# The mixers of a two-block transformer kernel: the written order of TensorE starts at the value projections, second-half gate values between the u blocks, spatial products last

## The chip, the cores and the metric

One core of a Trainium2 chip runs the whole kernel. The metric is the device time of one execution in microseconds (us), as the median of several runs. TensorE (PE) multiplies matrices into accumulator banks, VectorE (DVE) and ScalarE (ACT) read the banks and compute elementwise, GpSimd (POOL) computes elementwise on the main on-chip memory alone, SyncE (SP) issues the loads. Each engine works through its own queue in order and waits on semaphores for the others.

## The reference, cut to what matters

The kernel computes two stacked models in single precision for 512 tokens of width 1024. The change lies in the two layers of the second one, in the first part of each layer (here called the mixer):

```
a = rms_norm(h, pre_mix_g)
zq, zkc, zvc, zks, zvs, zkw, zvw, zg, zu, zv = split(a @ w_in)
q = rope(zq);  k_sel = rope(zks);  k_win = rope(zkw)
kc, vc = compress(zkc), compress(zvc)        # blocks of 32 tokens -> gelu(. @ w1 + b1) @ w2 + b2
kc = rope(kc)
attn = g0 * softmax(q kc) vc + g1 * softmax(q k_sel) v_sel + g2 * softmax(q k_win) v_win
u = gelu(zu);  v = layer_norm(gelu(zv))      # v: tokens x 512
mlp = u * (tril(w_s) @ v + b_s)              # per group of 64 columns, in chunks of 128 tokens
mix = concat(rms_norm(attn), rms_norm(mlp)) @ w_o
h = h + rms_norm(mix)
```

## The kernel before

Activations lie with features on partitions: a tile `[128, 8, 512]` holds 8 blocks of 128 features of 512 tokens. Each weight block (128 x 1024, 512 KB) is loaded, and split into a high part (`whi`, ScalarE, L246) and a rest (`wlo`, VectorE, L249). A product is three matmuls per pair of blocks (high x high, high x low, low x high): a block product is 8 steps of three matmuls, 24 in all.

`mixer_in` makes everything that the attention needs: first two token tiles of the gate values `v` (with GELU and layer norm in `gln_evac`), the keys, the compressed hidden layer `ph`, the queries, then the two value projections (`proj(12 + b)`) with their transposes (vtr), the hidden layer's GELU (`hb`) and transposes (htr), the compressed keys (pkc, then a chain of small operations to `kcst`) and compressed values (pvc to `vcz`), and the transposed attention gates (gtr to `gt`). Up to there a scheduler that works on a timeline of its own chooses the order of TensorE.

From there on TensorE's order is written out by hand: inside `manual_schedule` its instructions go out in the order in which the code issues them. What was issued before it can still be placed between them, and all other engines keep the scheduler's order. `nsa` goes through 16 attention units `(n, rp, b)`: query block `n` of 128 tokens (0 to 3), two head pairs `rp`, two branches `b`; here they are counted 0 to 15. Each unit issues scores of a first and a second group (L1558, L1560; VectorE takes the row maxima `nm`, ScalarE the exponentials, VectorE scales `p`), and transposes (pt, L571) and weighs (o, L580) the unit before. `nsa_compressed` (tile `pc`) comes once per query block.

Between these pieces `slot(ns)` issues *fill*: so many nominal nanoseconds of dense matmuls from the generator `fill`, with what was overdrawn carried on as a debt. A generator that yields `None` has nothing to give. The fill runs through `rest` (four u blocks with GELU; the remaining token tiles 2 and 3 of the gate values; first-half spatial products `spatial(i, 0)`), `rest2` (`spatial(i, 1)`), and the output projection's first half `out["half"]`. A step of three 512-column matmuls counts 681 ns, one of 256 columns 360 ns, a spatial product 1200 ns. `slot.side(...)` runs small steps, one for each slot: `mix_norm` squares and adds, lets some slots pass, and then issues the column sums (rsc, L312), a power on GpSimd (`rcol`, L316), transposes (rsb, L320) and the scaling. Matmul banks: two "mm", three "s", two "pt", one "o".

```
        def rest(wq, slot):                       # L1400
            for j in range(4):
                p = self.bk("mm", [128, S])
                yield from self.mm3_steps(p, next(wq), ax)
                self.gelu2(u[:, j, :], p, gp.tile([128, S], F32, name="gmt", tag="gmt", bufs=2))
                if j % 2:
                    yield spatial(j // 2, 0)
```

Of the kernel before, what the change touches and what calls it, by code (L numbers as in the profile page):

```python
# [10 lines left out]
F32 = mybir.dt.float32  # L11
# [3 lines left out]
AF = mybir.ActivationFunctionType  # L15
# [191 lines left out]
class _K:  # L207
# [927 lines left out]
    def mixer(self, l, at):  # L1135
# [11 lines left out]
        nc.gpsimd.memset(vcz, 0.0)  # L1147
        order = [d[f"w_in{l}"][2 + j] for j in range(4)] + [d[f"w_zv{l}"][0, k] for k in range(4)]
        order += [d[f"wo{l}"][m] for m in range(8)] * 2
        with ExitStack() as sl_, ExitStack() as sg:  # L1150
            gp = self.pool(sg, "mixg", side="right")
            with ExitStack() as s2:
                rest, rest2 = self.mixer_in(l, self.pool(s2, "mixe"), gp, u, qst, kst, kcst, vv, vcz, gt)
            lp = self.pool(sl_, "mixl")
            out = {}

            def fill(wq):
                yield from rest(wq, slot)
                while slot.sides or "ao" not in out:
                    yield None  # L1160
                yield from rest2(slot)
                sg.close()
                out["half"], out["after"] = self.mixer_out(l, self.pool(sl_, "mixf", side="right"))
                yield from out["half"](wq, HALVES[0])
                while "last" not in out:
                    yield None
                yield from out["half"](wq, HALVES[1])

            wq = self.wqueue(order)
            slot = _Slots(fill(wq))  # L1170
            with self.tc.manual_schedule(engines={mybir.EngineType.PE}):
                for hf in self.nsa(lp, qst, kst, kcst, vv, vcz, gt, cmask, slot):
                    slot.side(self.mix_norm(l, "attn_g", self.ao, 0, hf, True))
                    out["ao"] = True
# [19 lines left out]
                self.up = self.group([wu[i] for i in range(self.GROUP)], ("mm", "mm", "s", "s", "s", "pt", "pt"), slot=slot)  # L1194
                assert not slot.sides
        self.tap(f"hm{l}", self.h)

    GROUP = 7

    def mix_norm(self, l, gain, src, k0, hf, quick=False):  # L1200

# [23 lines left out]
    def mixer_in(self, l, at, gp, u, qst, kst, kcst, vv, vcz, gt):  # L1225
# [114 lines left out]
        for r in range(4):  # L1340
            q_ = roped(proj(8 + r) if r else gr[8], 0.125)
            compress(r)
            for g in range(2):
                x, y = (slice(0, 64), slice(64, 128)) if g == 0 else (slice(64, 128), slice(0, 64))
                nc.scalar.copy(qst[x, 2 * r + g, :], q_[x, :])
                nc.vector.tensor_sub(qst[y, 2 * r + g, :], q_[x, :], qst[x, 2 * r + g, :])
        for b in range(2):
            v_ = ev("v_")
            nc.scalar.copy(v_, proj(12 + b))
            p = ptt("vtr", [128, 4, 128])  # L1350
            for t in range(4):
                nc.tensor.transpose(p[:, t, :], v_[:, 128 * t:128 * t + 128], self.ident)
            nc.vector.tensor_copy(vv[b], p)
# [30 lines left out]

        def spatial(i, hf):

            p = self.bk("mm", [128, 2, 2, 128])
            for j in range(2):
                for c in range(2):
                    for e in range(2):  # L1390
                        g = 4 * i + 2 * j + e
                        nc.tensor.matmul(p[64 * e:64 * e + 64, j, c, :], v[:, 2 * hf + c, 64 * g:64 * g + 64], ws[:, g, :],
                                         start=True, stop=True)
            t = gp.tile([128, 2, 2, 128], F32, name="gmt", tag="gmt", bufs=2)
            nc.vector.tensor_tensor(t, p, bs[:, 2 * i:2 * i + 2, None, :].to_broadcast([128, 2, 2, 128]), op=ALU.add)
            x = u[:, 2 * i:2 * i + 2, HALVES[hf]].rearrange("p j (c t) -> p j c t", c=2)
            nc.gpsimd.tensor_mul(x, x, t)
            return 1200

        def rest(wq, slot):  # L1400
            for j in range(4):
                p = self.bk("mm", [128, S])
                yield from self.mm3_steps(p, next(wq), ax)
                self.gelu2(u[:, j, :], p, gp.tile([128, S], F32, name="gmt", tag="gmt", bufs=2))
                if j % 2:
                    yield spatial(j // 2, 0)
            slot.side(self.mix_norm(l, "mlp_g", u[:, :, HALVES[0]], 4, 0))
            pss = [self.bk("mm", [128, S]) for _ in range(2)]
            for kq in range(4):
                w = next(wq)  # L1410
                for t, p in zip((2, 3), pss):
                    for k2 in range(2):
                        k = 2 * kq + k2
                        for i, (a, b) in enumerate(((0, 0), (0, 1), (1, 0))):
                            nc.tensor.matmul(p, self.a[a][:, k, 128 * t:128 * t + 128], w[b][:, 512 * k2:512 * k2 + 512],
                                             start=k == 0 and i == 0, stop=k == 7 and i == 2)
                        yield 681
            for t, p in zip((2, 3), pss):
                gln_evac(t, 0, p)

        def rest2(slot):
            for i in range(2):
                yield spatial(i, 1)
            slot.side(self.mix_norm(l, "mlp_g", u[:, :, HALVES[1]], 4, 1))

        return rest, rest2

# [29 lines left out]
    def nsa(self, at, qst, kst, kcst, vv, vcz, gt, cmask, slot):  # L1457
# [5 lines left out]
        for unit in units + [None]:  # L1463
# [41 lines left out]

    FILL = (2700, 2700, 3400, 3000)

# [214 lines left out]
```

## Time and profile before

| | us |
|---|---|
| median of 3 runs | 2364.74 (2364.59 to 2366.53) |
| the profiled execution's own time | 2362.37 |
| its span | 2360.5 |
| TensorE busy in the span | 2237.1 |
| VectorE / ScalarE / GpSimd busy | 1701.1 / 1140.2 / 519.6 |

Times of rows are counted from the start of the span. PE is the matmuls, PEld the weight loads of TensorE, which run beside them. "idle before" is the time an engine stood still ahead of an instruction, with what ended it. The granted clock is 1.00 at 2.4 GHz and 0.50 at 1.2 GHz.

### The profile page before, as it was taken

Reading aid. Unit: us, or ns where it says so; the run is one execution under the profiler, and the core shown is the slowest. Engines: PE = TensorE matmul, PEld = TensorE weight load, DVE = VectorE, ACT = ScalarE, POOL = GpSimd, SP = SyncE. Lnnn points to the kernel's source line nnn. Section 1 sums busy time; section 2 is a strip of 40 time slices with the busy share of each in tenths; the row PEclk is TensorE's granted clock in tenths of the full one; section 3 lists DMA queues with packets and bytes.
Section 4 is the critical chain, followed back from the end, with each engine's and each line's share of the span. In section 5 each row is a group of like instructions: output and inputs, shape, how many; then the busy total and the mean of one; then the engine's idle time right before and its main releaser. Section 6 shows DMA issues by size and latency. Waiting matters only on the chain.

```text
span 2360.5 us, 37236 instructions
## 1 busy us (share of the span) xinstructions
PE 2237.1 (95%) x14372; PEld 1941.6 (82%) x14372; DVE 1701.1 (72%) x2922; ACT 1140.2 (48%) x2105; POOL 519.6 (22%) x556
## 2 busy tenths in 40 slices
PE   7999999999999989897999999999987999999998
PEld 5877788888888888665898889998865798888998
DVE  5898656846888878776787665668957688666558
ACT  3534444643443434455664444555445665444454
POOL 0110010312444344113121110133203131111004
PEclk9999999999999999998999999999988999999999
DMA  7443134432212344311253235655411143333664
GB/s 286 134 151 99 37 104 132 141 124 82 62 63 63 113 152 130 132 37 46 81 170 105 92 95 157 181 185 163 176 53 45 43 157 126 96 98 112 176 195 134
DMA packets 83746, 279.03 MB, mean 118 GB/s; under 512 B 9584, under 2 KB 14704, under 8 KB 83568
## 3 DMA queue, kind: packets, MB, share of 16 engines
q1 hardware_dynamic: 83568, 276.64, 36.7%
q8 instruction: 113, 1.85, 0.3%
q14 instruction: 65, 0.53, 0.1%
HBM read 274.51 MB, written 2.10 MB: 117 GB/s over the span
## 4 chain that ended last, share of the span: by engine, by line
PE 75%; DVE 13%; ACT 4%; issue 3%; POOL 3%; DMA 2%; SPq 0%; DVEq 0%; ACTq 0%; POOLq 0%
PE mm L279 28%; PE bg L279 23%; PE s L279 3%; DVE wlo L249 2%; PE o L580 2%; PE s L924 2%; PE pt L571 2%; PE bg L845 2%; PE pt L279 1%; PE s L1558 1%; DMA w<-in_w_ada 1%; ACT whi L246 1%; PE s L845 1%; PE bg L1659 1%; DVE ada_p L403 1%
## 5 line engine op out<-in xcount | busy, mean ns | idle before, releaser
L246 ACT CAST whi<-w 128x1024 fp32r<-128x1024 f32 (+1 forms) x436 | 449.1, 1033 | 555.5 <-PE mm L279 249.0
L249 DVE TENSOR_TENSOR wlo<-w,whi 128x1024 fp32r<-128x1024 f32 (+1 forms) x420 | 522.7, 1246 | 223.6 <-ACT whi L246 221.7
L279 PE MATMUL bg<-a,whi 128*128 128x512 f32 x1344 | 415.9, 391 | 0.2 <-ACT whi L246 0.2
L279 PEld LDWEIGHTS bg<-a,whi 128*128 128x128 f32 x1344 | 252.3, 188 | 54.6 <-ACT whi L246 1.0
L279 PE MATMUL mm<-hx,whi 128*128 128x512 f32 x864 | 275.6, 399 | 3.4 <-DVE sga L682 3.0
L279 PE MATMUL bg<-a,wlo 128*128 128x512 f32 x672 | 262.2, 391 | 2.0 <-DVE wlo L249 2.0
L279 PE MATMUL mm<-fh,whi 128*128 128x256 f32 x1408 | 252.7, 282 | 0.0
L279 PEld LDWEIGHTS mm<-fh,whi 128*128 128x128 f32 x1408 | 217.2, 189 | 0.2
L279 PE MATMUL mm<-fh,wlo 128*128 128x256 f32 x704 | 198.9, 284 | 0.6 <-DVE wlo L249 0.6
L279 PEld LDWEIGHTS mm<-hx,whi 128*128 128x128 f32 x864 | 157.9, 190 | 33.1 <-DVE sga L682 3.2
L279 PE MATMUL mm<-a,whi 128*128 128x256 f32 (+1 forms) x768 | 169.8, 317 | 0.0
L279 PE MATMUL mm<-hx,wlo 128*128 128x512 f32 x432 | 169.7, 393 | 0.0
L279 PEld LDWEIGHTS bg<-a,wlo 128*128 128x128 f32 x672 | 126.6, 188 | 29.8 <-DVE wlo L249 3.1
L1611 POOL TENSOR_TENSOR cv<-cv 128x512 f32<-128x512 f32 x44 | 61.5, 1398 | 386.2 <-DVE cv L1598 386.2
L1598 DVE SCALAR_TENSOR_TENSOR cv<-q,cols,cv 128x511 f32<-128x511 f32 (+1 forms) x176 | 134.5, 767 | 2.5
L279 PEld LDWEIGHTS mm<-fh,wlo 128*128 128x128 f32 x704 | 132.6, 189 | 1.0 <-DVE wlo L249 1.0
L279 PEld LDWEIGHTS mm<-a,whi 128*128 128x128 f32 x768 | 124.0, 196 | 7.1 <-issue 4.2
L1605 DVE TENSOR_TENSOR q<-bg,rr 128x512 f32<-128x512 f32 x74 | 51.1, 691 | 107.6 <-PE bg L279 107.6
L279 PE MATMUL mm<-a,wlo 128*128 128x256 f32 (+1 forms) x384 | 117.8, 307 | 0.6 <-DVE wlo L249 0.6
L279 PE MATMUL mm<-hc,whi 128*128 128x256 f32 x576 | 108.6, 287 | 2.3 <-ACT k L813 2.2
L316 POOL TENSOR_TENSOR rcol<-rcol,mhalf 128x2 f32<-128x2 f32 x33 | 24.3, 736 | 348.4 <-DVE rcol L315 348.4
L571 PE MATMUL pt<-ident,p 128*128 128x128 f32 x496 | 72.8, 285 | 29.4 <-DVE p L1577 20.8
(465 smaller groups left out, 4999.8 us busy)
## 6 DMA issues: line engine op xcount, KB each, us to landing
w<-in_wup SPq DMA_DIRECT2D x102, 512.0 KB, 3.5
w<-in_wdn SPq DMA_DIRECT2D x64, 448.0 KB, 3.5
w<-in_w_ada SPq DMA_DIRECT2D x48, 512.0 KB, 3.7
w<-in_w_c SPq DMA_DIRECT2D x48, 512.0 KB, 3.5
w<-in_w_in SPq DMA_DIRECT2D x38, 512.0 KB, 4.7
w<-in_wo SPq DMA_DIRECT2D x32, 512.0 KB, 3.5
w<-in_wdn SPq DMA_DIRECT2D x32, 512.0 KB, 3.6
w<-in_wpg SPq DMA_DIRECT2D x32, 512.0 KB, 3.8
```

Of the source, the lines that this page charges most:

```text
L246: self.nc.scalar.copy(hi[:, :c], w)
L249: eng.tensor_sub(lo[:, :c], w, hi[:, :c])
L279: self.nc.tensor.matmul(ps, w[a][:, (k - k0) * c:(k - k0 + 1) * c], x[b](k), start=first and n == 0, stop=last and n == 3 * len(ks) - 1)
L316: nc.gpsimd.tensor_tensor(col, col, self.mhalf[:, :nt], op=ALU.pow)
L403: nc.vector.scalar_tensor_tensor(t, w, 1.0, self.srow[i], op0=ALU.mult, op1=ALU.mult, accum_out=sums[:, j, i:i + 1])
L571: nc.tensor.transpose(pt[:, c:c + 128], P[g][:, i, kb * 128:(kb + 1) * 128], self.ident)
L580: self.nc.tensor.matmul(o[64 * g:64 * g + 64, 2 * rp:2 * rp + 2, :].rearrange("p a b -> p (a b)"), vt[:, keys[kb], 64 * g:64 * g + 64], pb ...
L845: nc.tensor.matmul(p, xf(k, a, t), w[b][:, 512 * k2:512 * k2 + 512], start=k == 0 and i == 0, stop=k == 7 and i == 2)
L924: nc.tensor.matmul(s_[:, c, :], lhs(c), rhs(c), start=True, stop=True)
L1598: nc.vector.scalar_tensor_tensor(t[:, s:], p[:, :S - s], cw(i), t[:, s:], op0=ALU.mult, op1=ALU.add)
L1605: nc.vector.tensor_mul(q, p, self.rr)
L1611: nc.gpsimd.tensor_mul(a, a, b)
```

## The change

The written order now begins before the value projections, and their two banks are taken from "s"; htr, vtr, pkc, pvc and gtr follow in a fixed order, with two slots of 1300 ns of fill behind the value transposes. The fill goes u0, u1, gate values of tiles 2 and 3, u2, u3, then all four spatial products; `rest2` is gone, and the output projection starts once the side steps of both mlp halves are over. Unit 0's second slot is 4500 instead of 3500, the third entry of `FILL` 4000 instead of 3400. `mix_norm` waits two slots instead of three for the mlp halves and the first attention half, four for the second. Four multiplications by 0.5 on GpSimd (`w2k`, `w2v`, `tri`, `bs`) go; `ht` is copied with a scale of 0.5, and the mlp half, now twice as large, is normalised with four times the epsilon.

```diff
-        order = [d[f"w_in{l}"][2 + j] for j in range(4)] + [d[f"w_zv{l}"][0, k] for k in range(4)]
+        order = [d[f"w_in{l}"][2 + j] for j in (0, 1)] + [d[f"w_zv{l}"][0, k] for k in range(4)]
+        order += [d[f"w_in{l}"][2 + j] for j in (2, 3)]
         order += [d[f"wo{l}"][m] for m in range(8)] * 2
...
-            def fill(wq):
+            def fill(rest):
+                wq = self.wqueue(order)
                 yield from rest(wq, slot)
                 while slot.sides or "ao" not in out:
                     yield None
-                yield from rest2(slot)
                 sg.close()
...
+            with ExitStack() as s2:
+                steps = self.mixer_in(l, self.pool(s2, "mixe"), gp, u, qst, kst, kcst, vv, vcz, gt)
+                slot = self.slot = _Slots(fill(next(steps)))
+                region = self.tc.manual_schedule(engines={mybir.EngineType.PE})
+                region.__enter__()
+                now(steps)
...
-                    slot.side(self.mix_norm(l, "attn_g", self.ao, 0, hf, True))
+                    slot.side(self.mix_norm(l, "attn_g", self.ao, 0, hf, True, 4 if hf else 2))
...
-    def mix_norm(self, l, gain, src, k0, hf, quick=False):
+    def mix_norm(self, l, gain, src, k0, hf, quick=False, wait=2):
-        for _ in range(3):
+        for _ in range(wait):
             yield
-        pr = yield from self.rstd_steps([sq[0][:, 0, :]], 256, self.mean512, NORM_EPS, tmp, "pt")
+        pr = yield from self.rstd_steps([sq[0][:, 0, :]], 256, self.mean512, NORM_EPS * (1 if quick else 4), tmp, "pt")
...
-        for w2 in (w2k, w2v):
-            nc.gpsimd.tensor_scalar(w2, w2, 0.5, None, op0=ALU.mult)
-        nc.gpsimd.tensor_scalar(tri, tri, 0.5, None, op0=ALU.mult)
         nc.gpsimd.tensor_mul(ws, ws, tri[:, None, :].to_broadcast([128, 8, 128]))
-        nc.gpsimd.tensor_scalar(bs, bs, 0.5, None, op0=ALU.mult)
...
+        def rest(wq, slot):
+            def ublock(j):
+                p = self.bk("mm", [128, S])
+                yield from self.mm3_steps(p, next(wq), ax)
+                self.gelu2(u[:, j, :], p, gp.tile([128, S], F32, name="gmt", tag="gmt", bufs=2))
+            for j in range(2):
+                yield from ublock(j)
+            pss = [self.bk("mm", [128, S]) for _ in range(2)]
...
+            for t, p in zip((2, 3), pss):
+                gln_evac(t, 0, p)
+            for j in range(2, 4):
+                yield from ublock(j)
+            for hf in range(2):
+                for i in range(2):
+                    yield spatial(i, hf)
+                slot.side(self.mix_norm(l, "mlp_g", u[:, :, HALVES[hf]], 4, hf))
+        yield rest
+        pv = []
         for b in range(2):
-            v_ = ev("v_")
-            nc.scalar.copy(v_, proj(12 + b))
-            p = ptt("vtr", [128, 4, 128])
...
+            pv.append(proj(12 + b, lambda: self.bk("s", [128, S])))
         hb = at.tile([128, 256], F32, name="hb")
...
+        vs = [ev("v_") for _ in range(2)]
+        nc.scalar.copy(vs[0], pv[0])
         p = ptt("htr", [128, 2, 128])
...
-        nc.scalar.copy(ht, p)
+        nc.scalar.activation(ht, p, AF.Copy, scale=0.5)
+        nc.scalar.copy(vs[1], pv[1])
+        for b in range(2):
+            p = ptt("vtr", [128, 4, 128])
+            for t in range(4):
+                nc.tensor.transpose(p[:, t, :], vs[b][:, 128 * t:128 * t + 128], self.ident)
+            nc.vector.tensor_copy(vv[b], p)
+            self.slot(1300)
         p = ptt("pkc", [128, 64])
...
-                slot(fill if last else 3500)
+                slot(fill if last else 4500)
...
-    FILL = (2700, 2700, 3400, 3000)
+    FILL = (2700, 2700, 4000, 3000)
```

## Rows read from the trace of the kernel before

**Rows 1.** The page: span, and busy time of each engine.

```profile
span 2360.5 us, 37236 instructions
...
PE 2237.1 (95%) x14372; PEld 1941.6 (82%) x14372; DVE 1701.1 (72%) x2922; ACT 1140.2 (48%) x2105; POOL 519.6 (22%) x556
```

**Rows 2.** Stretches of both mixers: length, busy us (instructions), clock, DMA share, GB/s.

```profile
968.75:1155.10 186.35, 158.37 (x1055) 119.30 (x1056) 123.82 (x285) 102.02 (x248) 35.36 (x39) 0.93 0.18 57
1703.54:1889.90 186.36, 157.84 (x1058) 119.21 (x1058) 123.04 (x284) 102.28 (x249) 35.12 (x39) 0.93 0.17 57
```

**Rows 3.** Waits of TensorE in the first mixer: total us, times, longest.

```profile
PE mm L1392 <- POOL v L1296: 11.1, 2, 7.2
PE pt L571 <- DVE p L1577: 10.1, 4, 6.5
...
PE mm L1415 <- DVE gmt L1395: 0.8, 1, 0.8
```

**Rows 4.** Stretches of the first mixer: three holes, each followed by low clock.

```profile
990.90:997.85 6.95, 0.43 (x6) 0.35 (x5) 4.25 (x18) 3.73 (x14) 0.00 (x0) 0.80 0.17 64
997.85:1002.00 4.15, 4.15 (x15) 3.49 (x15) 1.50 (x8) 1.39 (x5) 0.00 (x0) 0.52 0.00 0
...
1010.40:1013.31 2.91, 0.00 (x1) 0.01 (x1) 2.91 (x8) 1.22 (x6) 1.26 (x1) 0.79 0.39 139
1013.31:1018.90 5.59, 5.59 (x19) 3.80 (x19) 3.65 (x16) 2.22 (x7) 1.34 (x2) 0.50 0.00 0
...
1077.70:1089.50 11.80, 0.69 (x4) 0.29 (x4) 7.15 (x18) 3.09 (x5) 9.18 (x10) 0.61 0.14 44
1089.50:1093.80 4.30, 4.30 (x24) 2.81 (x24) 1.25 (x2) 0.64 (x2) 1.27 (x1) 0.50 0.00 0
```

**Rows 5.** The same stretches of the second mixer.

```profile
1726.46:1733.55 7.09, 0.01 (x2) 0.03 (x1) 4.34 (x20) 3.73 (x14) 0.00 (x0) 0.67 0.13 51
1733.55:1738.60 5.05, 5.05 (x19) 3.79 (x19) 2.25 (x11) 1.39 (x5) 0.00 (x0) 0.50 0.00 0
...
1746.78:1749.70 2.92, 0.00 (x0) 0.00 (x1) 2.92 (x8) 1.23 (x6) 1.26 (x1) 0.95 0.37 149
1749.70:1752.50 2.80, 2.80 (x12) 2.57 (x13) 1.29 (x5) 1.63 (x4) 0.67 (x1) 0.50 0.00 0
...
1812.90:1824.66 11.76, 0.69 (x5) 0.30 (x5) 7.11 (x18) 3.08 (x5) 9.14 (x10) 0.56 0.16 45
1824.66:1829.00 4.34, 4.34 (x32) 3.06 (x34) 1.57 (x3) 0.67 (x2) 1.28 (x1) 0.63 0.00 0
```

**Rows 6.** Timeline of TensorE, first mixer: start, busy us, operation, idle before.

```profile
883.05 0.69 PE L320 MATMUL rsb<-ident,rcol 128*128 128x128 f32 x2 [2.72 <-POOL rcol L316]
...
979.36 0.56 PE L1558 MATMUL s<-kst,qst 128*128 128x128 f32 x4
...
989.42 0.55 PE L1364 MATMUL pkc<-ht,w2k 128*128 128x64 f32 x4
...
1061.65 0.59 PE L1558 MATMUL s<-kst,qst 128*128 128x384 f32 x2
...
1070.30 0.60 PE L571 MATMUL pt<-ident,p 128*128 128x128 f32 x4
...
1152.81 0.58 PE L312 MATMUL rsc<-mean,msq 128*128 128x1 f32 x4 [1.49 <-DVE msq L1207]
```

**Rows 7.** Timeline of VectorE, first mixer.

```profile
993.33 0.22 DVE L254 TENSOR_TENSOR kcst<-kc,kcst 128x64 fp32r<-128x64 f32 x1 [0.31 <-ACT kcst L253]
993.47 1.08 DVE L1562 TENSOR_REDUCE nm<-s 128x2 f32<-128x256 f32 x3
...
1046.93 3.07 DVE L1577 TENSOR_SCALAR p<-p,sm 128x256 f32<-128x256 f32 x4
...
1065.39 1.08 DVE L1577 TENSOR_SCALAR p<-p,sm 128x384 f32<-128x384 f32 x3
```

**Rows 8.** Chain that ended last: the value projections.

```profile
968.75 10.77 PE bg L279 x46
```

**Rows 9.** Timeline of GpSimd: a sum of squares of the mlp half.

```profile
1047.72 1.33 POOL L1206 TENSOR_TENSOR msq<-msq 128x512 f32<-128x512 f32 x1
```

More of the change, by code (lines that the diff above doesn't have):

```diff
@@ L1151, in mixer @@
             gp = self.pool(sg, "mixg", side="right")
-            with ExitStack() as s2:
-                rest, rest2 = self.mixer_in(l, self.pool(s2, "mixe"), gp, u, qst, kst, kcst, vv, vcz, gt)
-            lp = self.pool(sl_, "mixl")
             out = {}
-            def fill(wq):
+            def fill(rest):
+                wq = self.wqueue(order)
                 yield from rest(wq, slot)
@@ L1167, in fill @@
                 yield from out["half"](wq, HALVES[1])
-            wq = self.wqueue(order)
-            slot = _Slots(fill(wq))
-            with self.tc.manual_schedule(engines={mybir.EngineType.PE}):
+            with ExitStack() as s2:
[4 more added lines that the diff above has]
+                now(steps)
+            lp = self.pool(sl_, "mixl")
+            if True:
                 for hf in self.nsa(lp, qst, kst, kcst, vv, vcz, gt, cmask, slot):
-                    slot.side(self.mix_norm(l, "attn_g", self.ao, 0, hf, True))
+                    slot.side(self.mix_norm(l, "attn_g", self.ao, 0, hf, True, 4 if hf else 2))
                     out["ao"] = True
@@ L1195, in mixer @@
                 assert not slot.sides
+                region.__exit__(None, None, None)
         self.tap(f"hm{l}", self.h)
     GROUP = 7
-    def mix_norm(self, l, gain, src, k0, hf, quick=False):
+    def mix_norm(self, l, gain, src, k0, hf, quick=False, wait=2):
         nc, tmp = self.nc, self.nrm
@@ L1346, in mixer_in, with spatial @@
                 nc.vector.tensor_sub(qst[y, 2 * r + g, :], q_[x, :], qst[x, 2 * r + g, :])
-        for b in range(2):
-            v_ = ev("v_")
-            nc.scalar.copy(v_, proj(12 + b))
-            p = ptt("vtr", [128, 4, 128])
-            for t in range(4):
-                nc.tensor.transpose(p[:, t, :], v_[:, 128 * t:128 * t + 128], self.ident)
-            nc.vector.tensor_copy(vv[b], p)
+        def spatial(i, hf):
+            p = self.bk("mm", [128, 2, 2, 128])
+            for j in range(2):
+                for c in range(2):
+                    for e in range(2):
+                        g = 4 * i + 2 * j + e
+                        nc.tensor.matmul(p[64 * e:64 * e + 64, j, c, :], v[:, 2 * hf + c, 64 * g:64 * g + 64], ws[:, g, :],
+                                         start=True, stop=True)
+            t = gp.tile([128, 2, 2, 128], F32, name="gmt", tag="gmt", bufs=2)
+            nc.vector.tensor_tensor(t, p, bs[:, 2 * i:2 * i + 2, None, :].to_broadcast([128, 2, 2, 128]), op=ALU.add)
+            x = u[:, 2 * i:2 * i + 2, HALVES[hf]].rearrange("p j (c t) -> p j c t", c=2)
+            nc.gpsimd.tensor_mul(x, x, t)
+            return 1200
@@ new lines, in rest @@
+        def rest(wq, slot):
[3 more added lines that the diff above has]
+                self.gelu2(u[:, j, :], p, gp.tile([128, S], F32, name="gmt", tag="gmt", bufs=2))
+            for j in range(2):
+                yield from ublock(j)
+            pss = [self.bk("mm", [128, S]) for _ in range(2)]
+            for kq in range(4):
+                w = next(wq)
+                for t, p in zip((2, 3), pss):
+                    for k2 in range(2):
+                        k = 2 * kq + k2
+                        for i, (a, b) in enumerate(((0, 0), (0, 1), (1, 0))):
+                            nc.tensor.matmul(p, self.a[a][:, k, 128 * t:128 * t + 128], w[b][:, 512 * k2:512 * k2 + 512],
+                                             start=k == 0 and i == 0, stop=k == 7 and i == 2)
+                        yield 681
+            for t, p in zip((2, 3), pss):
+                gln_evac(t, 0, p)
[5 more added lines that the diff above has]
+                slot.side(self.mix_norm(l, "mlp_g", u[:, :, HALVES[hf]], 4, hf))
@@ L1383, in mixer_in @@
         nc.vector.tensor_scalar(gt, p, 0.5, 0.5, op0=ALU.mult, op1=ALU.add)
[L1385 to L1426, printed above, removed]
     def mixer_out(self, l, at):
```

## Prediction, made before the changed kernel ran

> **What bounds the kernel now.** The page comes first: the span is 2360.5 us [rows 1] and the profiled run, with what lies around the span, took 2362.37 us. The diff touches only the two mixers, so the view of stretches by engine was asked next. From the first value projection to the transposes of the last normalisation a mixer takes 186.4 us, TensorE is busy for 158 of them, VectorE for 124, ScalarE for 102 and GpSimd for 35, and the DMA engines are used to 0.18 [rows 2]. TensorE is thus the engine with most to do, and what it does not do in these stretches is lost. The view of waits says where: 11.1 us for the gate values `v` (two waits) and 10.1 us for the attention weights `p`; the rest is small [rows 3]. The stretches around these waits then give each hole and what follows it: TensorE is idle, and when work returns it runs for some microseconds at the lower of its two clock levels, 1.2 GHz (granted 0.50 to 0.63) [rows 4, 5]. A hole costs its idle time plus, of the busy time behind it, the part that the clock withheld (busy times one minus granted).
>
> Hole A, before the first transposes of `p`: 6.95-0.43 = 6.5 idle and 4.15 x 0.48 = 2.0 of clock in the first mixer, 7.1 and 5.05 x 0.50 = 2.5 in the second; together 18.1 us. Hole B, one head pair later: 2.9 + 5.59 x 0.50 = 5.7, and 2.9 + 2.80 x 0.50 = 4.3; together 10.0. Hole C, the two second-half spatial products: 11.80-0.69 = 11.1 and 4.30 x 0.50 = 2.15; 11.1 and 4.34 x 0.37 = 1.6; together 26.0. A last wait of 1.5 stands ahead of the last normalisation's column sums [rows 6], the same in both mixers: 3.0. All of it is 57.1 us.
>
> **The change, part by part.** *Start of the written order.* Before, the first scores went out at 979.36, but pkc, the first product of the compressed keys, only at 989.42 [rows 6], as it had no place in the written order and was fitted in between. VectorE reduced the first scores (nm) at 993.47, directly behind the last split of the compressed keys at 993.33 [rows 7]: its queue is served in order, and the whole chain of `kc` stood ahead. So the softmax that TensorE waits for in hole A was held up by pkc. After, htr, vtr, pkc, pvc and gtr come straight behind the 48 matmuls of the projections; 46 such matmuls took 10.77 us, 0.70 for a step of three [rows 8]. From the projections' end (about 979) to pkc there are htr, two vtr and four steps of fill: 4 us; the `kc` chain took 993.33-989.42 = 3.9 us, so the first nm comes near 988. Between the second scores and the transposes the new slots hold ten steps (1 of u0, 7 of u1, then 1 of u1 and 1 of the gate values), 7 us, where eight stood. A softmax takes 3.7 us from its scores to `p` (scores 1061.65 and a twin, over by 1062.8; `p` scaled by 1065.39 + 1.08) [rows 6, 7]. About 3 us stay in hand for VectorE's other work. I take hole A as gone. Nothing is added by the transposes' new place; TensorE issues all of them before too. What waits behind htr if `hb` is late is all of TensorE's list; two projections (10.8 us) cover that chain.
>
> *u0, u1, gate values, u2, u3, four spatial products.* In the nominal prices of the code a u block is 8 x 0.68 = 5.4, the gate values 16 x 0.68 = 10.9, a spatial product 1.2: 37.5 us in all, as before. The slots now give 2.6 (value transposes) + 2.0 + 4.5 + 0.9, then 2.7 a unit, 4.0 a unit in the third block. Counted through, u1 ends in unit 1, the gate values in unit 5, u3 in unit 8, the spatial products in unit 9. Normalising `v` thus has two u blocks and three attention units over it, over 20 us, against the 12 us that hole C shows it needs. Hole C goes. Hole B goes for the most part: its spatial addition, GELU and GpSimd product are elsewhere now, while one split of weights and the compressed scores stay; 0 to 2.9 can be left, I take 0.7 a mixer.
>
> *What comes instead.* (1) Banks: the gate values' second tile, u2 and the second spatial product each take a matmul bank two to five steps after a GELU began to empty it. The like place before cost 0.8 [rows 3]; below 0, above 2.9 as hole B; 3 x 0.8 = 2.4. (2) Unit 10 is left without fill: all fill but the output projection is used up, and that has to wait until both normalisations of the mlp half are through (three slots, 4 us). The attention's own work between second scores and transposes is then near 5.5 us (1061.65 to 1070.30 was 8.6, with some 3 us of fill [rows 6]), against 3.7 for a softmax in the clear. VectorE has four spatial additions, the compressed softmax and the attention half's normalisation there too, and GpSimd its products and sums. Where GpSimd ran, scaling four `p` of 256 columns took 3.07 us (1047.72 is one of its sums), where it did not, three of 384 took 1.08: 3.0 against 0.94 ns a column [rows 7, 9]. Between 0 (the softmax is in time) and 13 (hole C over again) I take 3.5, nearer the clear row, since the surplus of VectorE work is a few microseconds. (3) Column sums of the mlp normalisations now wait for two slots, not three, and the output projection's first block reads the mlp half soon after it: 0 to 3, taken 1. (4) At the end, 12 steps of 0.36 nominal stand ahead of the column sums where eight stood, so the 1.5 goes; but only three stand behind the transposes where ten did: 0 to 1.5, taken 0.5. Sum 8.1 a mixer, 16.2.
>
> *GpSimd's four halvings.* They go; the factor moves into a copy that exists and into an epsilon. In the first mixer two of them stand ahead of a GpSimd power for which TensorE waits 2.72 [rows 6]: gain 0 to 2.7, taken 1.4. In the second nothing waits for them: 0. The SP queue issues the same weight loads in another order, each at least one block ahead of its use; at a DMA share of 0.18 [rows 2] that costs nothing, and with the cover gone one block would wait for one landing.
>
> Sum: 57.1 - 16.2 + 1.4 = 42.3 us less. From the profiled run that is 2320; the median shown is 2.4 us above that run, so 2322.
>
> The Trainium skill, page "SBUF — State Buffer", section "Who interferes with whom", says that VectorE and GpSimd share one pair of ports as an exclusive lock, which the loser waits out. The `p` scaling above agrees (3.07 us beside GpSimd's work). By that rule the clustered GpSimd products would hold VectorE up in just the unit without fill, which speaks against the change; the first rival below is what it would give.
>
> **The rivals.** *Hole C reappears in the unit without fill.* GpSimd's four products, four sums and eight scalings, once in two places, meet the spatial additions and two softmaxes in some 20 us; VectorE at three times the time a column cannot keep up, and TensorE waits 10 us there plus 2 of clock. For it: the 3.07 row. Against: the same GpSimd work exists before and takes only 35 us of 186. Price: 12 in place of 3.5, 17 more in both mixers: 2339.
>
> *Hole A stays.* The queues of the other engines keep an order in which the first reductions stand behind something late (a GELU, a second value copy). For it: just that happened before. Against: pkc, on which it hung, is now written ahead of the scores. Price 18: 2340.
>
> *All waits go.* Only hole-free attention, with nothing of (1) to (4): 2322 - 16 = 2306.
>
> *The attention chain is the bound, waits only move.* If scores, softmax, transposes, weighing in series set the time, every hole closed opens elsewhere, and the first scores are issued about 5.4 us later (behind the transposes and four steps). It decides once the first reduction comes later than 993.5 of the old clock. Price 2 x 5.4 = 11: 2376, slower. Against it: VectorE idles for 62 of 186 us, ScalarE for 84 [rows 2], and outside the holes TensorE is busy almost throughout. If the chain is the bound and starts no later: no change, 2365.
>
> **How the numbers follow.** Forecast 0.58 (its own range 2311 to 2333), hole C again 0.14, hole A stays 0.10, all waits go 0.08, waits move and start later 0.06, waits move only 0.04. The time given is the forecast's. The range takes in the first, second and third cases and the best: 2304 to 2344; 0.1 of the slower cases and a rest of 0.05 lie outside. A measurement of this kernel can tell 0.2%, 4.7 us. Faster by more: 0.58 + 0.14 + 0.10 + 0.08 = 0.90, a little of it lost to both rivals at once: 0.89. Within: 0.04. Slower: 0.07.
>
> **What would show it.** Right: the first nm comes within about 9 us of the projections' end and no wait of several microseconds stands before the first transposes; no wait for `v` at the spatial products; u2 and u3 stand between the gate values and them; the mixer stretches of [rows 2] last 163 to 168 us, with full clock but for one short dip; and waits on a GELU or on `p` in the middle of the mixer add up to a few microseconds. Wrong: a hole before the transposes of unit 9 or 10 as long as hole C, nm again behind the `kc` chain and late, or a mixer stretch near 186 us with waits on ScalarE or VectorE spread through it.

## The result, and the profile after

| | us |
|---|---|
| before, median of 4 runs | 2365.64 (2364.59 to 2368.63) |
| changed, median of 4 runs | 2333.89 (2333.01 to 2340.36) |
| ratio | 0.987, 95% interval 0.9849 to 0.989 |

The change is faster by 31.8 us; forecast were 2322, in a range of 2304 to 2344. The profile after is that of the slowest of the four executions. Its span and the busy times, to be held against [rows 1]:

```profile
span 2338.6 us, 37220 instructions
...
PE 2244.5 (96%) x14372; PEld 1948.9 (83%) x14372; DVE 1707.5 (73%) x2922; ACT 1140.5 (49%) x2105; POOL 510.6 (22%) x548
```

The stretches of [rows 2] end at a transpose that now has another amount of dense work ahead of it. A fair stretch has the same work in it: from the end of `ph` to the first matmul of the up projection that goes into a bank of transposes, in both mixers. The view of stretches, with length, busy times of PE, PEld, DVE, ACT, POOL, granted clock, DMA share and GB/s, for the kernel before:

```profile
967.84:1200.84 233.00, 203.85 (x1430) 163.94 (x1430) 165.03 (x349) 136.56 (x313) 49.83 (x49) 0.94 0.24 75
1703.60:1936.95 233.35, 203.89 (x1429) 164.85 (x1429) 163.40 (x348) 135.83 (x313) 49.56 (x49) 0.93 0.23 75
```

and for the changed one:

```profile
973.54:1191.36 217.82, 203.97 (x1430) 165.09 (x1429) 165.00 (x349) 135.92 (x313) 48.28 (x49) 0.97 0.26 81
1693.84:1913.60 219.76, 205.99 (x1430) 166.14 (x1429) 166.75 (x348) 135.19 (x313) 47.46 (x49) 0.95 0.26 80
```

A mixer is 15.2 and 13.6 us shorter, with nearly the same busy time on every engine. TensorE stood idle for 29.1 and 29.5 us (length minus busy) and now for 13.9 and 13.8: in this profile all of the gain is idle time.

The start of the first mixer, TensorE's timeline of the changed kernel (start, duration; in brackets idle time and its releaser):

```profile
984.51 0.38 PE L1400 MATMUL htr<-ident,hb 128*128 128x128 f32 x2
...
988.39 0.55 PE L1412 MATMUL pkc<-ht,w2k 128*128 128x64 f32 x4
...
989.79 0.66 PE L1564 MATMUL s<-kst,qst 128*128 128x128 f32 x4
...
1000.41 0.60 PE L571 MATMUL pt<-ident,p 128*128 128x128 f32 x4
...
1004.50 0.50 PE L1377 MATMUL mm<-whi,a 128*128 128x512 f32 x1 [1.35 <-DVE u L262]
```

and VectorE's:

```profile
991.70 0.23 DVE L254 TENSOR_TENSOR kcst<-kc,kcst 128x64 fp32r<-128x64 f32 x1 [0.31 <-ACT kcst L253]
991.84 0.42 DVE L1568 TENSOR_REDUCE nm<-s 128x2 f32<-128x256 f32 x1
...
997.62 0.88 DVE L1583 TENSOR_SCALAR p<-p,sm 128x128 f32<-128x128 f32 x4
```

pkc now stands ahead of the scores, the first `nm` comes 7.3 us behind the projections' end (984.5), where before it came 14 behind it [rows 6 to 8], and `p` is ready at 998.5, 1.9 us before its transposes, which no longer wait. The waits of TensorE in the first mixer (total us, times, longest), against [rows 3]:

```profile
PE pt L571 <- DVE p L1583: 2.3, 4, 1.5
PE pt L571 <- ACT a L253: 1.8, 1, 1.8
PE rsb L320 <- POOL rcol L316: 1.8, 2, 1.3
PE rsc L312 <- POOL msq L1212: 1.7, 1, 1.7
PE mm L1377 <- DVE u L262: 1.4, 1, 1.4
```

The two waits of 11.1 and 10.1 are gone, and no wait for `v` is left. In their place stand small ones, most of them in unit 10, which has no fill. TensorE's timeline there:

```profile
1068.62 0.56 PE L312 MATMUL rsc<-mean,msq 128*128 128x1 f32 x4
1070.96 0.63 PE L571 MATMUL pt<-ident,p 128*128 128x128 f32 x4 [1.78 <-ACT a L253]
1072.32 0.66 PE L571 MATMUL pt<-ident,p 128*128 128x128 f32 x4 [0.73 <-ACT ptS L267]
...
1074.39 0.43 PE L320 MATMUL rsb<-ident,rcol 128*128 128x128 f32 x2 [0.51 <-POOL rcol L316]
...
1078.89 0.61 PE L312 MATMUL rsc<-mean,msq 128*128 128x1 f32 x4 [1.65 <-POOL msq L1212]
...
1083.00 0.69 PE L320 MATMUL rsb<-ident,rcol 128*128 128x128 f32 x2 [1.25 <-POOL rcol L316]
```

Five waits, 5.9 us together. What they and the others do to the clock is seen in the stretches (the column behind the five busy times), against [rows 4]:

```profile
984.45:1000.41 15.96, 15.96 (x94) 13.45 (x92) 9.58 (x28) 7.92 (x18) 0.00 (x0) 1.00 0.35 100
...
1002.49:1009.00 6.51, 5.16 (x25) 4.15 (x25) 3.13 (x11) 3.09 (x10) 0.00 (x0) 0.74 0.25 81
1004.50:1009.00 4.50, 4.50 (x21) 3.95 (x21) 1.47 (x6) 1.85 (x5) 0.00 (x0) 0.62 0.11 44
...
1033.00:1040.00 7.00, 5.55 (x36) 3.81 (x35) 5.37 (x18) 2.63 (x9) 4.49 (x5) 1.00 0.12 50
...
1146.00:1160.00 14.00, 12.78 (x90) 12.18 (x89) 10.75 (x17) 7.06 (x15) 6.00 (x5) 0.88 0.42 146
```

Where hole A was, TensorE is busy without a gap at full clock. But behind the 1.35 us wait for a bank, behind unit 10 and at the mixer's end (two waits of 0.5 for the first halves' normalisation) the lower level comes back: three times in the first mixer, and four times in the second. Not every wait does this. Behind one of 1.45 us for `p` (1033.34 to 1034.80) the clock stays at 1.00, and so it does in another execution of the same kernel (e1_again, below) behind the same wait for a bank:

```profile
995.33:1001.84 6.51, 5.16 (x32) 3.87 (x34) 4.26 (x12) 2.95 (x10) 0.00 (x0) 1.00 0.26 81
```

### The profile page after: what moved, and what is told of

It reads as the page before. It is cut to its first block, busy times and chain, and to the rows that moved or that the text cites. A ratio compares the mean times of both kernels' runs of the same rounds, so it can differ in the third digit from the quotient of the medians.

```text
span 2338.6 us, 37220 instructions
## 1 busy us (share of the span) xinstructions
PE 2244.5 (96%) x14372; PEld 1948.9 (83%) x14372; DVE 1707.5 (73%) x2922; ACT 1140.5 (49%) x2105; POOL 510.6 (22%) x548
## 4 chain that ended last, share of the span: by engine, by line
PE 76%; DVE 15%; ACT 3%; issue 3%; DMA 2%; POOL 2%; SPq 0%; DVEq 0%; ACTq 0%; POOLq 0%
PE mm L279 29%; PE bg L279 23%; PE s L279 4%; DVE wlo L249 3%; PE o L580 2%; PE s L924 2%; PE pt L571 2%; PE bg L845 2%; DMA w<-in_w_ada 2%; PE s L1564 1%; PE pt L279 1%; PE s L845 1%; PE bg L1665 1%; ACT whi L246 1%; PE mm L1377 1%
## 5 line engine op out<-in xcount | busy, mean ns | idle before, releaser
L279 PE MATMUL bg<-a,whi 128*128 128x512 f32 x1280 | 395.7, 391 | 0.0
L279 PEld LDWEIGHTS bg<-a,whi 128*128 128x128 f32 x1280 | 240.4, 188 | 51.2 <-issue 1.0
L279 PE MATMUL bg<-a,wlo 128*128 128x512 f32 x640 | 249.7, 391 | 2.6 <-DVE wlo L249 2.6
L279 PEld LDWEIGHTS bg<-a,wlo 128*128 128x128 f32 x640 | 120.6, 188 | 29.0 <-DVE wlo L249 4.0
L279 PE MATMUL s<-a,whi 128*128 128x256 f32 (+1 forms) x576 | 116.4, 300 | 1.6 <-DVE a L254 1.6
L279 PEld LDWEIGHTS s<-a,whi 128*128 128x128 f32 x576 | 92.9, 194 | 5.6 <-DVE a L254 1.9
```

The costliest lines, as they stand in the source:

```text
L279: self.nc.tensor.matmul(ps, w[a][:, (k - k0) * c:(k - k0 + 1) * c], x[b](k), start=first and n == 0, stop=last and n == 3 * len(ks) - 1)
```

## The experiments

Kernels of one group ran on one chip beside runs of the kernel before. The table has the measured median and ratio, and from the profile of each, both mixers together: the length of the stretch just defined, TensorE's idle time in it, and what the low clock withheld (busy times one minus granted, summed over pieces of 2 us).

| kernel | median us | ratio, 95% interval | length | idle | clock |
|---|---|---|---|---|---|
| before | | | 466.4 | 58.6 | 15.4 |
| changed | 2333.89 | 0.987, 0.9849 to 0.989 | 437.6 | 27.6 | 15.2 |
| e1_again (group 1) | 2332.41 | 0.9855, 0.9841 to 0.9868 | 435.7 | 28.8 | 12.2 |
| e2_halvings_only (1) | 2362.06 | 0.998, 0.9971 to 0.9989 | 466.4 | 58.9 | 15.9 |
| e3_order_only (1) | 2356.53 | 0.9958, 0.9945 to 0.997 | 451.2 | 48.0 | 7.5 |
| e4_fill_only (1) | 2347.24 | 0.9919, 0.9905 to 0.9932 | 445.7 | 42.4 | 7.7 |
| e5_halvings_back (2) | 2340.14 | 0.9893, 0.9877 to 0.9909 | 438.8 | 27.8 | 16.9 |
| e6_early_half (2) | 2332.56 | 0.986, 0.9844 to 0.9876 | 431.7 | 27.6 | 7.9 |
| e7_mm_banks (2) | 2330.99 | 0.9861, 0.984 to 0.9882 | 433.8 | 24.0 | 15.8 |
| e8_idle_fill (2) | 2328.72 | 0.9848, 0.9828 to 0.9869 | 431.6 | 20.3 | 8.4 |
| e9_changed_again (3) | 2334.94 | 0.9863, 0.9845 to 0.9881 | 436.2 | 29.1 | 12.3 |
| e10_tile2_first (3) | 2335.89 | 0.9869, 0.9853 to 0.9885 | 437.0 | 28.2 | 14.5 |
| e11_three (3) | 2329.36 | 0.9841, 0.9825 to 0.9857 | 429.8 | 27.7 | 6.3 |
| e12_four (3) | 2343.82 | 0.9902, 0.9886 to 0.9917 | 445.4 | 32.1 | 16.3 |

The kernel before had medians of 2367.55, 2363.7 and 2365.77 in the three groups, so ratios are compared, not times. One profile's span differs from another's of the same kernel by some microseconds ahead of the mixers (see the end), so single spans are not compared either.

**The parts alone.** First the changed kernel unaltered, to know the spread:

> The changed kernel once more, unchanged, for a second profile: its first profiled execution (2340.4 us) was the slowest of its four. Theory (the 6 us lie in one place outside the change, such as a load that came late): a profile near 2333 us, with mixer stretches as in the first profile (173 and 177 us). Rival (the mixers themselves vary): one of the mixer stretches some 6 us shorter. Ratio to before 0.985 to 0.989 by both.

The theory was right that the difference lies outside the change, but not in one place: of the 8.3 us between the two profiled executions 1.9 lie in the mixer stretches and 7.2 ahead of the first mixer (see the end).

Then the kernel before without the four halvings (with the scaled copy and epsilon):

```diff
-        for w2 in (w2k, w2v):
-            nc.gpsimd.tensor_scalar(w2, w2, 0.5, None, op0=ALU.mult)
-        nc.gpsimd.tensor_scalar(tri, tri, 0.5, None, op0=ALU.mult)
...
-        nc.gpsimd.tensor_scalar(bs, bs, 0.5, None, op0=ALU.mult)
```

> The kernel before with only the four GpSimd halvings taken out (scale in the copy of ht, four times the epsilon for the mlp half). In the changed kernel the first mixer's value projections began 5.7 us later than before, although no instruction ahead of them was added. Theory (without the halvings the other engines' queues are ordered differently ahead of the first mixer, to its loss): value projections some 4 to 6 us later, 2367 to 2371 us. Rival (the late start comes from the new written order): no change, within 2 us of before, or 1 to 3 us less by the shorter wait for GpSimd's power.

It gains 0.2%, 2.6 to 6.9 us by its interval, and its mixer stretches are as long as before: what it gains lies outside them. The theory of a late start falls (`ph` ended at 966.4, before at 967.8); the gain is more than the rival gave it. Next, the kernel before with the written order of TensorE beginning at the value projections, the fill, slots and side steps as before:

```diff
-            wq = self.wqueue(order)
-            slot = _Slots(fill(wq))
-            with self.tc.manual_schedule(engines={mybir.EngineType.PE}):
+                slot = self.slot = _Slots(fill(next(steps)))
+                region = self.tc.manual_schedule(engines={mybir.EngineType.PE})
+                region.__enter__()
+                now(steps)
```

> The kernel before with only the first part of the change: the written order begins at the value projections, with their two banks from s, htr, vtr, pkc, pvc, gtr in fixed order and two slots of 1300; fill order, slot sizes, halvings and waiting slots as before. Theory (this part alone closes hole A, 18 us over both mixers, and leaves holes B and C): 2345 to 2351 us, no wait over 1 us ahead of the first transposes of p, hole C of 11 us in both mixers. Rival (the holes hang together; the fill that now runs earlier is missing later): 2356 to 2366 us, with hole C or B longer by what A gave.

Ratio 0.9958, 10 us of 2366: by the time the rival was right, though no hole grew by as much as hole A gave. Hole A is gone, but the waits of its first mixer show hole C longer than before [rows 3] and a new one for a bank of transposes:

```profile
PE mm L1360 <- POOL v L1302: 12.6, 2, 9.5
PE pt L1551 <- DVE ptS L267: 3.8, 1, 3.8
...
PE pt L571 <- DVE p L1588: 1.3, 3, 0.6
```

Then the other part, the kernel before with the new order of fill (u0, u1, gate values, u2, u3, spatial products last) and nothing else:

```diff
-            for j in range(4):
...
-                if j % 2:
-                    yield spatial(j // 2, 0)
+            for j in range(2):
+                yield from ublock(j)
...
+            for j in range(2, 4):
+                yield from ublock(j)
+            for hf in range(2):
+                for i in range(2):
+                    yield spatial(i, hf)
```

> The kernel before with only the second part: fill in the order u0, u1, gate values, u2, u3, four spatial products; everything else as before. Theory (this closes hole C and most of B, 36 us, and opens a hole in the unit without fill): 2337 to 2347 us, hole A of 6.5 to 7 us still there, no wait for v. Rival (the unit without fill costs as much as hole C): 2353 to 2365 us.

Ratio 0.9919, 19 us: 2347.24, at the upper end of the theory's range. No wait for `v` is left, and hole A stands as it did, the 6.5 in the row of `p`:

```profile
PE pt L571 <- DVE p L1582: 11.1, 5, 6.5
PE mm L1416 <- DVE u L262: 1.5, 1, 1.5
```

So holes A and C belong to the parts that the prediction gave them to. Hole B does not: the prediction gave it to the order of fill, but the third transposes of `p`, ahead of which it stood, wait in neither kernel (1012.54 in e3, 1015.71 in e4). Either part alone removes it:

```profile
1012.54 0.60 PE L571 MATMUL pt<-ident,p 128*128 128x128 f32 x4
...
1015.71 0.60 PE L571 MATMUL pt<-ident,p 128*128 128x128 f32 x4
```

By the medians the parts add up: 4.7 + 10 + 19 make the 34 us that the ratio of e1_again gives in the same group. In the mixers they do not. There e3 and e4 save 15.2 and 20.7 us, 35.9 in all, and the changed kernel 28.8 to 30.7. The low clock shows it most: each part alone leaves 7.5 to 7.7 us of it, half of what it was before, and the two together leave 12.2 to 15.2. Last, the halvings put back into the changed kernel:

```diff
+        for w2 in (w2k, w2v):
+            nc.gpsimd.tensor_scalar(w2, w2, 0.5, None, op0=ALU.mult)
+        nc.gpsimd.tensor_scalar(tri, tri, 0.5, None, op0=ALU.mult)
...
+        nc.gpsimd.tensor_scalar(bs, bs, 0.5, None, op0=ALU.mult)
```

> The changed kernel with the four halvings put back on GpSimd (and the epsilon and the copy as before). Alone, their removal was worth 4.7 us, more than the 1.4 that the prediction gave it. If the four halvings cost as much behind the new order, this is 4 to 5 us slower than the changed kernel of the call before (2332), so 2336 to 2337, ratio 0.987. Rival: with the new order nothing waits for them, and it stays at 2332.

0.9893 against 0.987, 0.9855 and 0.9863 for the changed kernel in its own runs: 5 to 9 us by the middle values, at least as much as alone. The intervals overlap, but on the same chip all four times (2338.57 to 2342.39) lie above all of e6, e7 and e8 below, which have no halvings (2325.92 to 2336.97). The rival falls. Where the time lies is not settled: the stretch between the two mixers took 506.9 us, against 502.1 to 503.2 in the three profiles of the changed kernel, but the kernel before has 502.8 there with its halvings.

**Unit 10 and the low clock.** Three alterations of the changed kernel, one each. The output projection's first half may start earlier (`done` is filled by the side steps):

```diff
-                while slot.sides or "ao" not in out:
+                while "mlp0" not in self.done or "attn0" not in self.done:
                     yield None
...
-                yield from self.mm3_steps(p, next(wq), [lambda k, t=t: t[:, k, sl] for t in self.a], (4, 5, 6, 7, 0, 1, 2, 3))
+                yield from self.mm3_steps(p, next(wq), [lambda k, t=t: t[:, k, sl] for t in self.a],
+                                          (4, 5, 6, 7, 0, 1, 2, 3) if sl.start else range(8))
```

> The changed kernel, but the output projection's first half may start as soon as the first halves of both normalisations are through (the second mlp half need not be), and goes through the attention half's blocks first. Theory: the waits of the attention unit without fill (1.8 for a bank of transposes, 0.7, 0.5, 1.7 and 1.3 around the normalisations) and the low clock behind them are there because TensorE has no dense work for them; fill in two of the three empty slots takes 3 to 5 us a mixer: 2323 to 2327, ratio 0.983. Rival: the chains on VectorE and GpSimd set the length of that unit; then the waits only go to the output projection's first blocks, and it stays at 2330 to 2334.

The normalisations' banks:

```diff
-        pr = yield from self.rstd_steps([sq[0][:, 0, :]], 256, self.mean512, NORM_EPS * (1 if quick else 4), tmp, "pt")
+        pr = yield from self.rstd_steps([sq[0][:, 0, :]], 256, self.mean512, NORM_EPS * (1 if quick else 4), tmp, "pt" if quick else "mm")
```

> The changed kernel, with the column sums and transposes of the mlp normalisations in the banks of the dense products instead of the two of the transposes of p. Theory: the 1.8 us wait of the transposes in the unit without fill is for such a bank, held until the normalisation has been read; it goes, and some of the low clock behind it: 1 to 3 us a mixer, 2326 to 2330, ratio 0.983 to 0.985. Rival: the side steps themselves are what is late; the wait moves to them and the time stays at 2332.

And matmuls nobody reads:

```diff
+                p = self.bk("mm", [128, 256])
                 while slot.sides or "ao" not in out:
-                    yield None
+                    for _ in range(3):
+                        nc.tensor.matmul(p, self.a[0][:, 0, 256:384], self.a[0][:, 1, 256:512], start=True, stop=True)
+                    yield 360
```

> The changed kernel, with matmuls whose result nobody reads (three of 256 columns a step of 0.36) in the slots that have no fill to give, some 4 us of such steps in each mixer. Theory: TensorE waits there in any case, and its clock falls behind the waits (4.4 and 7.8 us of it in the two mixers); with the slots filled the waits shrink by what the steps take and the clock holds: between 0 and 6 us faster in all, 2326 to 2332. Rival: TensorE is the bound even there: 8 us slower, 2340.

None of the three can be told from the changed kernel by its ratio (0.9848 to 0.9861 against 0.9855 and 0.9863), so by the time alone e6 and e7 read as their rivals said, and e8 as its theory. The profiles say more. e7 loses 4 to 5 us of idle time and gets the low clock in return (15.8): its wait for the bank is 1.3, now on `nt`, instead of 1.8. It moved the banks of the mlp normalisations; `nt` is the scaling of the attention half's, whose bank stayed where it was. e6 keeps its idle time and has 7.9 us of low clock where the changed kernel has 12 to 15. e8 is the telling one. From the first column sums of the mlp half to its last transposes, and the 5.5 us behind, the changed kernel:

```profile
1068.62:1083.00 14.38, 8.46 (x56) 5.78 (x55) 13.16 (x31) 9.04 (x23) 9.49 (x11) 0.91 0.00 0
1083.00:1088.50 5.50, 5.50 (x29) 5.18 (x30) 4.07 (x9) 4.05 (x11) 4.30 (x6) 0.62 0.02 3
```

and e8:

```profile
1069.88:1084.46 14.58, 12.64 (x86) 10.12 (x86) 12.64 (x31) 8.45 (x22) 9.20 (x11) 0.88 0.00 1
1084.46:1089.96 5.50, 5.50 (x47) 4.68 (x46) 5.03 (x12) 4.76 (x13) 4.16 (x6) 1.00 0.00 0
```

TensorE has 30 more matmuls and 4.2 us more of busy time, and the stretch is 0.2 us longer. It was not what set the length there; VectorE, busy for 13.2 and 12.6 of these 14.4 and 14.6 us, is the engine nearest to full. And behind the stretch the clock is 1.00 where it was 0.62. In and behind unit 10 of both mixers the clock withheld 7.4, 7.2 and 5.9 us in the three profiles of the changed kernel, and 1.7 in e8.

**Tile 2 first, and the alterations together.** The 1.35 us wait for a bank, by letting tile 2 of the gate values take two weight blocks before tile 3 begins:

```diff
-            for kq in range(4):
-                w = next(wq)
+            for kqs in ((0, 1), (2,), (3,)):
+                ws_ = [next(wq) for _ in kqs]
                 for t, p in zip((2, 3), pss):
+                    for kq, w in zip(kqs, ws_):
```

> The changed kernel once more, unaltered, so that the other runs of this call can be held against it on the same chip: 2331 to 2335, ratio 0.985 to 0.987.

> The changed kernel, with tile 2 of the second-half gate values taking the first two weight blocks before tile 3 begins, so that tile 3 asks for its bank six matmuls later. Theory: the wait of 1.4 for that bank is an ordering matter and goes, and the low clock that follows it with it: about 2 us a mixer in the stretches, 2328. Rival: TensorE is short of something else there (p of the unit beside it), and the wait only changes its name: no change, 2332.

The wait for the bank is gone, and a longer one stands first in the list:

```profile
PE pt L1547 <- POOL pc L1539: 2.8, 1, 2.8
```

Length 437.0 against 436.2: the rival was right, it only moved. The three together, then with the unread matmuls of e8 in the slots still empty:

> The changed kernel with three alterations together: the early output projection, the matmul banks for the mlp normalisations, and tile 2 first. The mixer stretches of the first two, run alone, were 1 to 3 us shorter than those of the changed kernel, while the whole time showed no difference. Theory: idle time and low clock that remain in the mixers come from these places and add up: 5 to 9 us less in all, 2323 to 2328, ratio 0.982. Rival: each alteration only moves waits, and the three together give no more than one: 2330 to 2333.

> The three alterations, and matmuls whose result nobody reads in the slots that still have no fill. Theory: less low clock in the second mixer, where such matmuls alone took it from 7.8 to 3.4: 2320 to 2326. Rival: with the early output projection few slots are empty, and the steps only cost their own time: 0 to 2 us slower than the three alone.

e11 is the best of the versions by the mixers, 6.4 us shorter than e9 (429.8 against 436.2). Its idle time is 27.7 against 29.1; the low clock makes the most of it, 6.3 against 12.3. Its median falls between the theory's range and the rival's. It is 5.6 below e9's, with overlapping intervals, so that it beats the changed kernel is likely and not shown. Part of its gain, and of e8's, is not from the alterations: in their second mixers a wait of unit 5 is short that was long in all three profiles of the changed kernel (next section). The stretch of e11 over unit 10, where the clock withheld 3.1 us in both mixers:

```profile
1065.25:1080.94 15.69, 12.35 (x80) 9.24 (x80) 12.93 (x31) 10.58 (x26) 10.25 (x12) 0.89 0.01 1
1080.94:1086.44 5.50, 5.50 (x45) 4.69 (x46) 5.43 (x13) 4.46 (x14) 3.81 (x5) 1.00 0.33 95
```

e12 missed both expectations: 14 us slower than e11. In its timeline the unread matmuls themselves wait, since the matmul bank that falls to them, now that the normalisations draw banks of the same kind, is still being read by a spatial addition:

```profile
1070.57 1.92 PE L1162 MATMUL mm<-a 128*128 128x256 f32 x9 [2.29 <-DVE gmt L1365]
1072.28 1.91 PE L571 MATMUL pt<-ident,p 128*128 128x128 f32 x8
```

Behind them in the queue stand the transposes of `p`, the scores and the normalisation. From its first column sums to the last transposes (1067.71 to 1085.62) it takes 17.9 us, with six more matmuls than in e11, and the clock falls to its lower level again:

```profile
1082.80:1088.20 5.40, 5.40 (x23) 3.86 (x23) 2.91 (x8) 2.94 (x7) 2.10 (x4) 0.51 0.02 3
```

Over both mixers it has 4.4 us more of idle time than e11, which the two waits for that bank (2.29 in each mixer) would make up, and 10.0 more of low clock. Of these 10.0, 5.4 lie in and behind unit 10; the rest lies elsewhere, and one profile does not show that the bank is its cause. So what was free in e8 was not free here.

## Why the prediction was right, and where its size was off

*Hole A: right.* pkc, the first `nm` and the absent wait came as worked out (7.3 us behind the projections, with "within about 9" forecast; 1.9 us in hand for "about 3"). e3 and e4 show that the start of the written order does it and nothing else.

*Hole C: right.* Gone with the fill's order alone (e4); with the start of the order alone it grew to 12.6 (e3).

*Hole B: gone, but not for the reason given, and a wait came that the forecast did not have.* Ahead of the third transposes there is no wait any more, and either part alone does that (e3, e4). The waits for `p` that are left, 2.3 us in the first mixer and 3.7 in the second, stand for the most part ahead of unit 5's transposes, where VectorE has the GELU and the layer norm of the gate values to do:

```profile
1014.06 0.71 PE L571 MATMUL pt<-ident,p 128*128 128x128 f32 x4
...
1034.80 1.47 PE L571 MATMUL pt<-ident,p 128*128 128x128 f32 x8 [1.45 <-DVE p L1583]
...
1755.50 0.50 PE L571 MATMUL pt<-ident,p 128*128 128x128 f32 x2 [2.78 <-DVE p L1583]
```

The forecast counted the gate values up to unit 5 and took nothing there. The second mixer's wait is longer because there GpSimd multiplies `v` while VectorE scales `p`. The durations (shortest, median, longest, ns) of the four scalings, in the first mixer and in the second, and GpSimd's instructions beside the second:

```profile
L1583 DVE TENSOR_SCALAR p<-p,sm x4: 342/346/361, 1034.3 to 1035.1; 128x256 f32<-128x256 f32 x4
L1583 DVE TENSOR_SCALAR p<-p,sm x4: 340/828/1350, 1754.0 to 1756.8; 128x256 f32<-128x256 f32 x4
...
1753.95 1.26 POOL L1295 TENSOR_TENSOR v<-v,gln 128x512 f32<-128x512 f32 x1 [2.09 <-DVE v L1293]
...
1755.40 1.34 POOL L1296 TENSOR_TENSOR v<-v,gln 128x512 f32<-128x512 f32 x1
```

A scaling that started beside one of the two multiplications ended just behind it (1754.04 + 1.31 and 1755.54 + 1.35); the others took 0.34 as in the clear. So the price is one wait for each GpSimd instruction that is met, not so many ns a column. Whether they meet is a matter of timing: in both mixers of e8 and e11 they do not.

*New waits: near in sum, not in their places.* Of the three banks only the gate values' second tile waited (1.4 for 2.4). Unit 10 with its column sums was taken as 4.5 and idled 5.9 us. Part of that is a mechanism that the prediction did not have: the transposes of `p` waited 1.78 us for one of the two "pt" banks, which the attention half's normalisation held until VectorE had scaled from it, at 1070.81 (the profile names ScalarE's splits, which follow these scalings):

```profile
1069.17 1.64 DVE L1081 SCALAR_TENSOR_TENSOR nt<-ao,cols,rsb 128x256 f32<-128x256 f32 x4
```

The idle time saved was forecast as 22.0 - 8.1 in the first mixer and 22.6 - 8.1 in the second, 28.4 in all; the three profiles of the changed kernel have 31.0, 29.8 and 29.5. That it comes so near is partly luck: more was saved at the banks than forecast, and unit 5 and unit 10 took some of it back.

*The clock: this term failed.* The prediction let each closed hole give back the low clock behind it, 12.5 us in all, and charged the new waits with idle time alone. The low clock was 15.4 us before and is 15.2, 12.2 and 12.3 after: 0 to 3 came back. That is the greater part of what is missing: 42.3 us were forecast, and 31.8, 35.1 and 30.8 measured against the kernel before beside it. The rows that would have told were there: a hole of 11.1 us had 2.15 and 1.6 of low clock behind it, one of 2.9 had 2.8 and 1.4 [rows 4, 5]. In these rows it does not grow with the length of the hole. After, a wait of 1.35 has 4.50 x 0.38 = 1.7 behind it, unit 10's cluster 8.46 x 0.09 + 5.50 x 0.38 = 2.9, and the end of the mixer 12.78 x 0.12 = 1.5. Three new dips took the place of three old ones in the first mixer, and four of four in the second (there the last wait of 1.5 us before had low clock behind it too, which the forecast left out). For unit 10 e8 and e11 show that the new waits are the cause: with dense work in its slots 1.7 and 3.1 us are withheld there instead of 5.9 to 7.4. For the other dips it is argued from their place only: the same short wait has the low clock behind it in one execution and not in another. So the signs that the prediction named for the end came in part: not one short dip but three and four, and the stretches of [rows 2] not at 163 to 168 us but at 173 and 177, or, with the same work in them, 15.2 and 13.6 below 186.4.

The Trainium skill, page "TensorE: Matmul & The Clock Gate", section "HAM oscillation — how this bites in real kernels", says of a kernel in which TensorE waits for a load in every step of its loop that each step starts at the low clock, so that the transition is paid every time instead of once. The trace agrees for the holes of the kernel before: each of the three in each mixer has low clock behind it. Behind the shorter waits of the changed kernel it comes in some executions only. Where the dips only move, their price stays.

*Halvings: too small.* 1.4 was taken, with 2.7 as the upper bound in the first mixer and 0 in the second. Alone they were worth 2.6 to 6.9, in the changed kernel about 5 to 9. Where, stays open.

*The rivals.* Hole A did not stay, no wait moved as a whole, and the first scores did start about 5.3 us behind the projections' end without harm. "Hole C reappears in the unit without fill" (2339) was the nearest, and part right: the place was, and VectorE is the engine nearest to full there. Its measure was not: three `p` of 384 columns beside GpSimd's work took 1.51 and 1.97 us, 1.3 and 1.7 ns a column, between the clear 0.94 and the 3.0 that the rival assumed. One of the three was held up in the first case and two in the second, by GpSimd instructions that are shorter here (0.7 to 0.8 us) than in unit 5:

```profile
1067.74 1.51 DVE L1583 TENSOR_SCALAR p<-p,sm 128x384 f32<-128x384 f32 x3
...
1077.41 1.97 DVE L1583 TENSOR_SCALAR p<-p,sm 128x384 f32<-128x384 f32 x3
```

So the unit cost 5.9 + 2.9 = 8.8, with its column sums, between the 4.5 taken and the rival's 13 (12 and 1). The 3.0 itself was met, but in unit 5 of the second mixer.

## What to carry to other kernels

When holes are closed, look at the interruptions that are left or made, and not only at their microseconds: here waits of half a microsecond to two had the low clock behind them in some executions, and it then cost 1.5 to 3 us, as much as behind a hole of 7 or 11. A stretch whose length another engine sets is a place for dense work, wherever such work can be started early (e8 showed it to be free, e11 used it); but the banks that it takes must be free by then, or it becomes the obstacle itself (e12). An engine's instructions beside another's are worth a look one by one: here a slow group was one or two held up by a neighbour, and the rest as fast as ever. When work is reordered, compare stretches that hold the same work in both kernels.

## What the runs showed that was not expected

The part ahead of the mixers, in which TensorE's instructions have not been touched, ended (end of `ph`) at 966.4 to 974.8 us in fourteen profiles, without regard to the kernel: 973.5, 966.4 and 972.0 in three of the same changed kernel. A small part is the first load's landing (TensorE waits 7.4 or 5.6 us for it in the first two of these). The greater part is the granted clock: it withheld about 14 us there in the first and 7 in the second, by dips of which some are there in one execution and not in the next. From the second mixer's end on, the rest of the span was 424.8 to 425.0 us in twelve profiles of the fourteen.
